# Gate and up of a SwiGLU as 2x2 block products by Strassen's seven, in a float32 decoder layer on one core

## The chip, the core and the metric

The kernel runs on one core of a Trainium2 chip. TensorE (PE) multiplies, VectorE (DVE), ScalarE (ACT) and GpSimd (POOL) work beside it, SyncE (SP) issues most loads. The metric is the device time of one execution in microseconds; lower is better. The inputs are float32 and lie in the chip's main memory; so does the output.

## What is computed

One layer of a decoder on 256 tokens with 2048 columns: a SwiGLU with half weight, a mixer (four heads of differential attention, four of an mLSTM), a second SwiGLU with half weight, and a final norm. The change is in the two SwiGLUs and in what stands around them:

```python
def rmsnorm(x, g):
    x32 = x.astype(jnp.float32)
    y = x32 * lax.rsqrt(jnp.mean(x32 * x32, axis=-1, keepdims=True) + EPS)
    return (y * g.astype(jnp.float32)).astype(x.dtype)

def swiglu(h, w_gate, w_up, w_down):
    return (jax.nn.silu(h @ w_gate) * (h @ w_up)) @ w_down

# in reference(), with D_MODEL = 2048, D_FF = 5632:
x = x + 0.5 * swiglu(rmsnorm(x, ffn1_norm[l]), ffn1_w_gate[l], ffn1_w_up[l], ffn1_w_down[l])
...
x = x + jnp.concatenate([y_a, y_b], axis=-1) @ w_out[l]
x = x + 0.5 * swiglu(rmsnorm(x, ffn2_norm[l]), ffn2_w_gate[l], ffn2_w_up[l], ffn2_w_down[l])
return rmsnorm(x, final_norm)
```

## The kernel before

**Products.** PE multiplies float32 in float32r, a narrower form. To keep the accuracy, each operand is split in two: a high half, cast by ACT (`wh`, L112), and a low half, the rest, subtracted by DVE (`wl`, L113). A product is then three matmuls (`mm3`, L138 to L141): high by high, high by low, low by high. All three add into one PSUM tile `acc` of 128 tokens x 512 columns.

**Tiling.** `linear` computes both token halves of `x @ w` for 512 columns (a chunk). The 2048 rows of the weight are 16 contraction tiles of 128. They are loaded four at a time (1 MB, `raw`, by SP, L125) and split two at a time: a unit, 128 x 1024 elements for ACT and for DVE, is used by twelve matmuls (two contraction tiles, two token halves, three each). A gate chunk and an up chunk are 16 units, 192 matmuls. There are 11 chunks for each of the two SwiGLUs.

**The SwiGLU.** `swiglu` runs over the 11 chunks: gate (`ag`), Silu on ACT (`sg`), up (`au`), and on DVE `hidv`, the gated hidden rows of 128 tokens (L246). These must be transposed before they can be the stationary side of the down product. `hid_transposes` does that on PE (`tr`, eight transposes, L227), splits the result (`hidh` on ACT, `hidl` on DVE) and keeps all 44 transposed tiles until the down product, which runs over four chunks of 512 columns with 44 contraction tiles each and adds to `xres`, the residual.

**The order around the change.** Transposes are put off: they go on a list, `pending`, and `linear` calls `flush()` ahead of its unit FLUSH = 3, so that the last chunk's transposes come in one run between the units of the next product. The program is written in a straight line, and a scheduler places the instructions of each engine by priorities: what stands under `tc.high_priority(offset=AHEAD)` (loads and splits) may come up to 400 places ahead of its use, as far as tiles are free. From then on each engine has one fixed list. The tiles come from pools that rotate: three `raw` tiles, three pairs of `wh` and `wl`, four `acc`, 22 for the hidden halves.

**The head.** In the first chunk, x arrives transposed in eight pieces (`xraw`, L266), each with its split times the norm's gain (`split_gain`, L107 and L108) into `xt0h` to `xt3l`. The two loads of `xres` (L273) come after them. Where x changes later, `chunk_to_xt` transposes it on PE (L210) and splits it.

The functions that the change touches, and what calls them, with the line numbers of the profile:

Of the kernel before, what the change touches and what calls it, by code (L numbers as in the profile page):

```python
# [9 lines left out]
F32 = mybir.dt.float32  # L10
# [34 lines left out]
def tile_trunk_layer(ctx: ExitStack, tc: tile.TileContext, x, xt, par, bias_if, lamv, fnorm,  # L45
# [9 lines left out]
    ps_acc = ctx.enter_context(tc.tile_pool(name="ps_acc", bufs=4, space=PSUM))  # L55
    ps_tr = ctx.enter_context(tc.tile_pool(name="ps_tr", bufs=2, space=PSUM))
    ps_mx = ctx.enter_context(tc.tile_pool(name="ps_mx", bufs=2, space=PSUM))
# [8 lines left out]
    # constants  # L66
# [8 lines left out]
    for _ in range(WARM):  # L75
        # raises TensorE's clock while the first loads are under way
        nc.tensor.matmul(warm, zeros[:, 0:P], zeros, start=True, stop=True)
# [27 lines left out]
    def split_gain(src, gcol, hi, lo):  # L105
        """hi + lo = src * gain, each of float32r's width."""
        nc.scalar.activation(hi, src, AF.Copy, scale=prm[:, gcol:gcol + 1])  # L107
        nc.vector.scalar_tensor_tensor(lo, src, prm[:, gcol:gcol + 1], hi.bitcast(F32),  # L108
                                       op0=ALU.mult, op1=ALU.subtract)
# [9 lines left out]
    def load_w(src, pieces):  # L119
        """one load of LK contraction tiles of w, in pieces"""  # L120
# [17 lines left out]
    def mm3(acc, lh, ll, rh, rl, first, last):  # L138
        nc.tensor.matmul(acc, lh, rh, start=first, stop=False)  # L139
        nc.tensor.matmul(acc, lh, rl, start=False, stop=False)  # L140
        nc.tensor.matmul(acc, ll, rh, start=False, stop=last)  # L141
# [3 lines left out]
    def flush():  # L145
        """the transposes put off into the following products, where they come in one run"""
# [4 lines left out]
    def linear(xp, w, nk, last_units=1, ahead=None, in_pieces=False):  # L151
        """Both token halves of x @ w, w in units of UK contraction tiles, loaded LK at a time;
        xp[kt // 4] are pairs of [P, 4, S] tiles. The first half ends ahead of the second by last_units units."""
# [3 lines left out]
        def products(hb, u, rh, rl):  # L157
            sl = slice(hb * P, (hb + 1) * P)
            for t in range(UK):
                k = u * UK + t  # L160
                xh, xl = xp[k // 4]
                mm3(accs[hb], xh[:, k % 4, sl], xl[:, k % 4, sl], rh[:, t, :], rl[:, t, :],
                    k == 0, k == nk - 1)
# [3 lines left out]
        for u in range(nu):  # L167
# [5 lines left out]
            if o == 0:  # L173
                raw = load_w(w[u * UK // LK], (LK,) if not in_pieces else (UK, UK) if u else (1, 1, UK))
# [10 lines left out]
    def rsq(ssum, n, div, name):  # L185
        """(ssum / div + eps) ** -0.5 on [P, n]"""
# [6 lines left out]
    def square_sum(src, acc, scale=1.0):  # L193
        j = work.tile([P, CW], F32, tag="junk", name=nm("junk"), bufs=1)
# [7 lines left out]
    def chunk_to_xt(c, gbase, xp):  # L202
        """Transposes x's columns of chunk c into xp[c], times the norm's gain."""
        hi, lo = pair_tiles(big, f"xt{c}", [P, 4, S])
        xp[c] = (hi, lo)
        for j in range(0, 4, 2):
# [6 lines left out]
            for i in range(2):  # L213
                split_gain(tr[:, i, :], gbase + 4 * c + j + i, hi[:, j + i, :], lo[:, j + i, :])

    def residual(accs, c, scale, parts):
        for hb in range(NT):
            xs = xres[:, hb, c * CW:(c + 1) * CW]
            nc.vector.scalar_tensor_tensor(xs, accs[hb], scale, xs, op0=ALU.mult, op1=ALU.add)
            square_sum(xs, parts[:, hb, c:c + 1])  # L220
# [10 lines left out]
    def swiglu(xp, rstd, wg, wu, ahead=None):  # L231
        hid = []
        for c in range(F // CW):
            ag = linear(xp, wg[c], KD, ahead=ahead if c == 0 else None,
                        in_pieces=c == 0 and ahead is not None)
            r = rstd()
            sg = []
            for hb in range(NT):
                s = work.tile([P, CW], F32, tag="sg", name=nm("sg"))
                nc.scalar.activation(s, ag[hb], AF.Silu, scale=r[:, hb:hb + 1])  # L240
                sg.append(s)
            au = linear(xp, wu[c], KD)
            hs = []
            for hb in range(NT):
                h = work.tile([P, CW], F32, tag="hidv", name=nm("hidv"))
                nc.vector.scalar_tensor_tensor(h, au[hb], r[:, hb:hb + 1], sg[hb],  # L246
                                               op0=ALU.mult, op1=ALU.mult)
                hs.append(h)
            hi = hidp.tile([P, 4, S], F32R, tag="hid", name=nm("hidh"))
            lo = hidp.tile([P, 4, S], F32R, tag="hid", name=nm("hidl"))  # L250
# [5 lines left out]
    xp1 = {}  # L256

    def load_xt(u):
        k = u * UK
        c, o = k // 4, k % 4  # L260
        if o == 0:
            xp1[c] = pair_tiles(big, f"xt{c}", [P, 4, S])
        hi, lo = xp1[c]
# [465 lines left out]
```

## Time and profile before

| | |
|---|---|
| median of 3 runs | 1873.09 us (1873.05 to 1874.93) |
| the profiled execution, its span | 1870.5 us |
| PE, busy | 1859.7 us, 8456 instructions |
| DVE, busy | 955.4 us, 1031 instructions |
| ACT, busy | 846.4 us, 1019 instructions |
| POOL, busy | 10.0 us, 29 instructions |
| moved by DMA | 353.00 MB, 189 GB/s |

The span goes from the first instruction to the last in the profiler's record; the run's time has 2.6 us around that. In the chain of work that ended last, each step is followed back to what released it, so the engine with most of the chain is the one whose work sets the end. A row of the timeline gives start, duration, engine, line, operation, and the output tile and its inputs; in square brackets stands how long the engine was idle before, and for what. Matmuls are pipelined: their durations overlap, and the cost of one is the distance from start to start.

### The profile page before, as it was taken

Reading aid. Unit: us, or ns where it says so; the run is one execution under the profiler, and the core shown is the slowest. Engines: PE = TensorE matmul, PEld = TensorE weight load, DVE = VectorE, ACT = ScalarE, POOL = GpSimd, SP = SyncE. Lnnn points to the kernel's source line nnn. Section 1 sums busy time; section 2 is a strip of 40 time slices with the busy share of each in tenths; the row PEclk is TensorE's granted clock in tenths of the full one; section 3 lists DMA queues with packets and bytes.
Section 4 is the critical chain, followed back from the end, with each engine's and each line's share of the span. In section 5 each row is a group of like instructions: output and inputs, shape, how many; then the busy total and the mean of one; then the engine's idle time right before and its main releaser. Section 6 shows DMA issues by size and latency. Waiting matters only on the chain.

```text
span 1870.5 us, 20799 instructions
## 1 busy us (share of the span) xinstructions
PE 1859.7 (99%) x8456; PEld 1541.9 (82%) x8456; DVE 955.4 (51%) x1031; ACT 846.4 (45%) x1019; POOL 10.0 (1%) x29
## 2 busy tenths in 40 slices
PE   9999999999999999999999999999999999999998
PEld 7888888888888888978888888888888888888886
DVE  5455444545444454664465555444554445444554
ACT  7444444444444444554455554444444444434443
POOL 0000000000000000000000000000000000000000
PEclk9999999999999999999999999999999999999999
DMA  8555555555555555544544555555555555655553
GB/s 317 197 185 189 193 184 198 181 197 190 184 199 183 200 181 176 189 155 173 185 155 158 182 181 189 192 184 199 181 196 186 190 192 184 221 182 201 186 197 135
DMA packets 51935, 353.00 MB, mean 189 GB/s; under 512 B 6016, under 2 KB 6016, under 8 KB 11136
## 3 DMA queue, kind: packets, MB, share of 16 engines
q1 hardware_dynamic: 50544, 349.26, 51.9%
q10 hardware_dynamic: 1296, 2.42, 0.4%
q8 instruction: 66, 1.08, 0.2%
q14 instruction: 29, 0.24, 0.0%
HBM read 349.56 MB, written 2.10 MB: 188 GB/s over the span
## 4 chain that ended last, share of the span: by engine, by line
PE 98%; DMA 0%; ACT 0%; issue 0%; DVE 0%; POOL 0%; SPq 0%; POOLq 0%
PE acc L139 32%; PE acc L141 32%; PE acc L140 32%; PE tr L227 1%; PE tr L210 0%; DMA xraw<-in_xt_dram 0%; PE sc L547 0%; PE num L513 0%; PE tr L586 0%; PE tr L336 0%; PE rr L471 0%; PE tr L386 0%; PE st L480 0%; PE rr L473 0%; ACT junk L195 0%
## 5 line engine op out<-in xcount | busy, mean ns | idle before, releaser
L113 DVE TENSOR_TENSOR wl<-raw,wh 128x1024 fp32r<-128x1024 f32 (+2 forms) x665 | 805.0, 1211 | 872.8 <-ACT wh L112 872.3
L112 ACT CAST wh<-raw 128x1024 fp32r<-128x1024 f32 (+2 forms) x665 | 693.1, 1042 | 964.3 <-PE acc L141 955.4
L139 PE MATMUL acc<-wh,hidh 128*128 128x512 f32 x704 | 274.3, 390 | 0.0
L141 PE MATMUL acc<-wh,hidl 128*128 128x512 f32 x704 | 273.9, 389 | 0.0
L140 PE MATMUL acc<-wl,hidh 128*128 128x512 f32 x704 | 273.9, 389 | 0.0
L139 PE MATMUL acc<-wh,xt1h 128*128 128x512 f32 (+3 forms) x456 | 178.9, 392 | 0.0
L139 PE MATMUL acc<-wh,xt0h 128*128 128x512 f32 (+3 forms) x456 | 177.4, 390 | 0.3 <-ACT wh L112 0.2
L141 PE MATMUL acc<-wh,xt1l 128*128 128x512 f32 (+3 forms) x456 | 176.6, 387 | 0.0
L140 PE MATMUL acc<-wl,xt0h 128*128 128x512 f32 (+3 forms) x456 | 176.4, 387 | 0.0
L140 PE MATMUL acc<-wl,xt1h 128*128 128x512 f32 (+3 forms) x456 | 176.2, 386 | 0.0
L140 PE MATMUL acc<-wl,xt2h 128*128 128x512 f32 (+3 forms) x456 | 175.9, 386 | 0.0
L141 PE MATMUL acc<-wh,xt0l 128*128 128x512 f32 (+3 forms) x456 | 175.9, 386 | 0.0
L139 PE MATMUL acc<-wh,xt2h 128*128 128x512 f32 (+3 forms) x456 | 175.8, 386 | 0.0
L141 PE MATMUL acc<-wh,xt2l 128*128 128x512 f32 (+3 forms) x456 | 175.8, 386 | 0.0
L139 PE MATMUL acc<-wh,xt3h 128*128 128x512 f32 (+3 forms) x456 | 175.7, 385 | 0.0
L141 PE MATMUL acc<-wh,xt3l 128*128 128x512 f32 (+3 forms) x456 | 175.7, 385 | 0.0
L140 PE MATMUL acc<-wl,xt3h 128*128 128x512 f32 (+3 forms) x456 | 175.7, 385 | 0.0
L141 PEld LDWEIGHTS acc<-wh,hidl 128*128 128x128 f32 x704 | 132.2, 188 | 27.4
L139 PEld LDWEIGHTS acc<-wh,hidh 128*128 128x128 f32 x704 | 132.2, 188 | 27.3
L140 PEld LDWEIGHTS acc<-wl,hidh 128*128 128x128 f32 x704 | 132.2, 188 | 27.2
L139 PEld LDWEIGHTS acc<-wh,xt0h 128*128 128x128 f32 x456 | 85.7, 188 | 18.5 <-ACT wh L112 1.5
L140 PEld LDWEIGHTS acc<-wl,xt0h 128*128 128x128 f32 x456 | 85.7, 188 | 17.7 <-DVE wl L113 1.1
(199 smaller groups left out, 1575.5 us busy)
## 6 DMA issues: line engine op xcount, KB each, us to landing
raw<-in_wu_dram SPq DMA_DIRECT2D x88, 1024.0 KB, 4.8
raw<-in_wd_dram SPq DMA_DIRECT2D x88, 1024.0 KB, 4.8
raw<-in_wg_dram SPq DMA_DIRECT2D x84, 1024.0 KB, 4.8
raw<-in_win_dram SPq DMA_DIRECT2D x40, 1024.0 KB, 4.8
raw<-in_wout_dram SPq DMA_DIRECT2D x16, 1024.0 KB, 4.8
raw<-in_wg_dram SPq DMA_DIRECT2D x7, 512.0 KB, 7.7
raw<-in_wqk_dram SPq DMA_DIRECT2D x4, 784.0 KB, 4.4
raw<-in_wqk_dram SPq DMA_DIRECT2D x4, 768.0 KB, 4.4
```

What stands on the lines that cost most here:

```text
L112: nc.scalar.copy(hi, src)
L113: nc.vector.tensor_tensor(out=lo, in0=src, in1=hi.bitcast(F32), op=ALU.subtract)
L139: nc.tensor.matmul(acc, lh, rh, start=first, stop=False)
L140: nc.tensor.matmul(acc, lh, rl, start=False, stop=False)
L141: nc.tensor.matmul(acc, ll, rh, start=False, stop=last)
L227: nc.tensor.transpose(tr[:, i, hb * P:(hb + 1) * P], hs[hb][:, (j + i) * P:(j + i + 1) * P], ident)
```

## The change

Two contraction tiles (a pair) of x, by its two token halves, are taken as a 2x2 matrix of blocks A1, B1 (first tile) and A2, B2 (second tile); gate's and up's weights for these tiles are another. Their product, a 2x2 matrix too (two token halves by gate and up), is made by Strassen's scheme in Winograd's form: seven block products in place of eight, with four sums of x (`sums`, made once for a SwiGLU), four sums of the weights for each pair and chunk, and sums of the results. NP = 4 pairs, half of the 16 contraction tiles, are done so; the other eight remain plain. The first chunk of the first SwiGLU stays with `linear`.

In `paired`, a pair's gate and up tiles come by two loads of 512 KB into one `raw` tile. DVE makes two of the four weight sums into `f` (L305, 128 x 1024) and one into `raw` (L307, 128 x 512); the fourth is added by a DMA from SBUF to SBUF that accumulates (L354), issued by POOL. Four result tiles stay in PSUM, partial results are added on DVE and ACT (L338 to L341, L383, L386, L387). The SwiGLU's inner 5632 go in three parts of 4, 4 and 3 chunks: gate and up of a part, then its down product with 16, 16 and 12 contraction tiles, which adds to `xres` each time. Pools: 24 `slots` for hidden halves, x, its sums and `f` together, nine work tiles, four `raw`, four pairs of `wh` and `wl`, six `acc` (those of the mixer now among them).

PE's order within a paired chunk is: for each pair a unit u0 and a unit u1 of six matmuls (`prod0`, `prod1`); two units T of six, gate's second tile of two pairs times A2, each split in two pieces of 512; four units S of six, whose split reads the accumulated sum; and eight plain units of twelve, gate's contraction tiles 8 to 15, then up's, with loads of 1 MB.

The core of the diff; T, the plain units and what follows in the mixer (names of pools) are left out:

```diff
 UK = 2
+NP = 4
+PARTS = (4, 4, 3)
...
-    hidp = ctx.enter_context(tc.tile_pool(name="hidp", bufs=22))
-    wr = ctx.enter_context(tc.tile_pool(name="wr", bufs=3))
-    wsp = ctx.enter_context(tc.tile_pool(name="wsp", bufs=3))
-    work = ctx.enter_context(tc.tile_pool(name="work", bufs=2))
+    slots = ctx.enter_context(tc.tile_pool(name="slots", bufs=24))
+    work = ctx.enter_context(tc.tile_pool(name="work", bufs=9))
+    wr = ctx.enter_context(tc.tile_pool(name="wr", bufs=4))
+    wsp = ctx.enter_context(tc.tile_pool(name="wsp", bufs=4))
...
+    def sums(g):
+        for o, a, b, op in ((S1, B1, B2, ALU.subtract), (S3, A1, B1, ALU.subtract),
+                            (S2, S1, A1, ALU.subtract), (S4, A2, S2, ALU.add)):
+            nc.vector.tensor_tensor(out=g[:, o, :], in0=g[:, a, :], in1=g[:, b, :], op=op)
...
+    def paired(xp, wa, wb, nk, after_a):
+        n11, n21, n12, n22 = (ps_acc.tile([P, CW], F32, tag="acc", name=nm("acc")) for _ in range(4))
+        p1, p7, p5, p6 = n11, n21, n12, n22
...
+        def sums_first(j):
+            k = 2 * j
+            raw = wr.tile([P, 4, CW], F32, tag="raw", name=nm("raw"))
+            with tc.high_priority(offset=AHEAD):
+                nc.sync.dma_start(raw[:, 0:2, :], wa[k // LK][:, k % LK:k % LK + 2, :])
+                nc.sync.dma_start(raw[:, 2:4, :], wb[k // LK][:, k % LK:k % LK + 2, :])
+                f = slots.tile([P, 2, CW], F32, tag="s", name=nm("f"))
+                nc.vector.tensor_tensor(out=f, in0=raw[:, 0:4:3, :],
+                                        in1=raw[:, 2:3, :].to_broadcast([P, 2, CW]), op=ALU.add)
+                nc.vector.tensor_tensor(out=raw[:, 2, :], in0=f[:, 0, :], in1=raw[:, 3, :], op=ALU.add)
+                u0 = pair_tiles(wsp, "w", [P, 2, CW])
+                split(raw[:, 0:3:2, :], *u0)
+                u1 = pair_tiles(wsp, "w", [P, 2, CW])
+                split(f, *u1)
+            raws.append(raw)
+            return u0, u1
...
+        for j in range(NP):
+            if j == 2:
+                flush()
+            u0, u1 = sums_first(j)
+            prod0(j, u0)
+            held.append((j, u1))
+            if j != NP - 2:
+                for h in held:
+                    prod1(*h)
+                held.clear()
+        u2, u3, v = wk("u2"), wk("u3"), wk("v")
+        with soon():
+            nc.scalar.copy(u3, p1)
+            nc.vector.tensor_tensor(out=u2, in0=p6, in1=u3, op=ALU.add)
+            nc.vector.tensor_tensor(out=u3, in0=p7, in1=u2, op=ALU.add)
+            nc.vector.tensor_tensor(out=v, in0=p5, in1=u3, op=ALU.subtract)
...
+        for j in range(NP):
+            raw = raws[j]
+            with tc.high_priority(offset=AHEAD):
+                nc.gpsimd.dma_start(raw[:, 2, :], raw[:, 1, :], accum_op=ALU.add)
+                t = pair_tiles(wsp, "w", [P, 2, CW])
+                split(raw[:, 2:4, :], *t)
+            prod(n21, xp["pair", j], B2, t, 0, False, False, True)
+            prod(n12, xp["pair", j], S4, t, 1, False, False, True)
...
+    def ffn(xp, rstd, wg, wu, wd, finish, first=None):
+        done = 0
+        for part, n in enumerate(PARTS):
+            hid = hidden(xp, rstd, wg, wu, range(done, done + n), first)
+            for c in range(4):
+                finish(c, functools.partial(linear, dict(enumerate(hid)), wd[c], n * 4, w0=done), part,
+                       part == len(PARTS) - 1)
+            done += n
...
     def load_xt(u):
...
+            if u < NP:
+                g = gained(raw, G_FFN1 + k)
+                hi, lo = sum_tiles(xp1, u)
+                split(g[:, 0:4, :], hi[:, 0:4, :], lo[:, 0:4, :])
+                gs.append((g, hi, lo))
...
+        if u >= KD // UK - NP:
+            g, hi, lo = gs.pop(0)
+            sums(g)
+            split(g[:, 4:8, :], hi[:, 4:8, :], lo[:, 4:8, :])
```

**What moves.** The first place is DVE's list around the transposes of the last chunk's hidden rows. Before, in the second chunk of the first SwiGLU: the two `hidv`, four units of the weight, the two low halves of the transposes, the next unit.

```order
L246 SCALAR_TENSOR_TENSOR hidv_74_497<-acc_52_359,rstd_49_353,sg_50_355 128x512
L246 SCALAR_TENSOR_TENSOR hidv_75_499<-acc_53_360,rstd_49_353,sg_51_357 128x512
L113 TENSOR_TENSOR wl_87_542<-raw_85_539,wh_86_541 128x1024
L113 TENSOR_TENSOR wl_91_572<-raw_85_539,wh_90_571 128x1024
L113 TENSOR_TENSOR wl_94_590<-raw_92_587,wh_93_589 128x1024
L113 TENSOR_TENSOR wl_96_606<-raw_92_587,wh_95_605 128x1024
L113 TENSOR_TENSOR hidl_77_502<-tr_88_557,hidh_76_501 128x512
L113 TENSOR_TENSOR hidl_77_502<-tr_89_564,hidh_76_501 128x512
L113 TENSOR_TENSOR wl_99_624<-raw_97_621,wh_98_623 128x1024
```

After, in its fourth chunk: the two gated rows (`hv`), pair 1's second unit, the first low half, then the sums of pairs 2 and 3 (`f_247` and `raw_246`, `f_253` and `raw_252`), the second low half, pair 2's first unit.

```order
L278 SCALAR_TENSOR_TENSOR hv_224_1219<-u2_187_1001,rstd_57_383,sg_212_1145 128x512
L278 SCALAR_TENSOR_TENSOR hv_225_1221<-v_189_1003,rstd_57_383,sg_213_1147 128x512
L114 TENSOR_TENSOR wl_243_1266<-f_239_1258,wh_242_1265 128x1024
L114 TENSOR_TENSOR hidl_227_1224<-tr_244_1281,hidh_226_1223 128x512
L305 TENSOR_TENSOR f_247_1298<-raw_246_1295 128x1024
L305 TENSOR_TENSOR f_253_1318<-raw_252_1315 128x1024
L307 TENSOR_TENSOR raw_246_1295<-f_247_1298,raw_246_1295 128x512
L307 TENSOR_TENSOR raw_252_1315<-f_253_1318,raw_252_1315 128x512
L114 TENSOR_TENSOR hidl_227_1224<-tr_245_1288,hidh_226_1223 128x512
L114 TENSOR_TENSOR wl_249_1302<-raw_246_1295,wh_248_1301 128x1024
```

Between the low half of `tr_244` and that of `tr_245` now stand four sums that the next matmuls need; before, the two stood together, and the units ahead of them were those that PE used around its transposes.

The second place is PE's list at the same transposes. Before, from the fourth transpose to the first two matmuls of the unit behind them:

```order
L227 MATMUL tr_88_557<-ident_103,hidv_75_499 128x128
L227 MATMUL tr_89_564<-ident_103,hidv_74_497 128x128
L227 MATMUL tr_89_564<-ident_103,hidv_75_499 128x128
L227 MATMUL tr_89_564<-ident_103,hidv_74_497 128x128
L227 MATMUL tr_89_564<-ident_103,hidv_75_499 128x128
L139 MATMUL acc_78_503<-wh_90_571,xt1h_12_184 128x512
L140 MATMUL acc_78_503<-wl_91_572,xt1h_12_184 128x512
```

After, in the same way; `acc_228`, `acc_231` and `acc_229` are three of the chunk's four result tiles:

```order
L264 MATMUL tr_244_1281<-ident_100,hv_225_1221 128x128
L264 MATMUL tr_245_1288<-ident_100,hv_224_1219 128x128
L264 MATMUL tr_245_1288<-ident_100,hv_225_1221 128x128
L264 MATMUL tr_245_1288<-ident_100,hv_224_1219 128x128
L264 MATMUL tr_245_1288<-ident_100,hv_225_1221 128x128
L141 MATMUL acc_228_1225<-wh_248_1301,xs_18_191 128x512
L141 MATMUL acc_231_1228<-wh_248_1301,xs_18_191 128x512
L141 MATMUL acc_229_1226<-wh_250_1305,xs_18_191 128x512
L142 MATMUL acc_228_1225<-wl_249_1302,xs_18_191 128x512
```

The transposes stand between units as before, but what follows them (`wh_248`, `wh_250`) is now split from sums that DVE's list has behind the transposes' low half.

The third place is SP's list of loads in the first chunk. Before, its last x pieces and what follows:

```order
L266 DMA xraw_27_260<-in_xt_dram 128x512
L125 DMA raw_33_291<-in_wg1_dram 128x1024
L266 DMA xraw_32_284<-in_xt_dram 128x512
L125 DMA raw_33_291<-in_wg1_dram 128x1024
L266 DMA xraw_36_310<-in_xt_dram 128x512
L125 DMA raw_54_361<-in_wu1_dram 128x2048
L125 DMA raw_59_395<-in_wu1_dram 128x2048
L273 DMA xres_128<-in_x_dram 128x2048
L125 DMA raw_64_429<-in_wu1_dram 128x2048
L273 DMA xres_128<-in_x_dram 128x2048
```

After, from the first load of up's weights to the last x piece:

```order
L126 DMA raw_62_391<-in_wu1_dram 128x2048
L431 DMA xraw_23_214<-in_xt_dram 128x512
L126 DMA raw_67_425<-in_wu1_dram 128x2048
L452 DMA xres_125<-in_x_dram 128x2048
L431 DMA xraw_29_239<-in_xt_dram 128x512
L126 DMA raw_72_459<-in_wu1_dram 128x2048
L431 DMA xraw_35_272<-in_xt_dram 128x512
L431 DMA xraw_38_300<-in_xt_dram 128x512
L452 DMA xres_125<-in_x_dram 128x2048
L126 DMA raw_77_493<-in_wu1_dram 128x2048
L431 DMA xraw_44_334<-in_xt_dram 128x512
```

Up's weights (`in_wu1`) and x itself (`xres`) came behind the last piece of `xraw`; now four loads of the one and both of the other stand among and ahead of the pieces.

More of the change, by code (lines that the diff above doesn't have):

```diff
@@ L136, in split_w, with mm3, halves @@
         return hi, lo
[L138 to L141, printed above, removed]
+    def mm3(acc, lh, ll, rh, rl, first, last, on=False):
+        nc.tensor.matmul(acc, lh, rh, start=first, stop=False, skip_group_check=on)
+        nc.tensor.matmul(acc, lh, rl, start=False, stop=False, skip_group_check=on)
+        nc.tensor.matmul(acc, ll, rh, start=False, stop=last, skip_group_check=on)
+    def halves(xp, k, hb):
+        if ("pair", k // 2) in xp:
+            xh, xl = xp["pair", k // 2]
+            i = 2 * (k % 2) + hb
+            return xh[:, i, :], xl[:, i, :]
+        xh, xl = xp[k // 4]
+        sl = slice(hb * P, (hb + 1) * P)
+        return xh[:, k % 4, sl], xl[:, k % 4, sl]
     pending = []
@@ L229, in hid_transposes, with wk @@
             split(tr, hi[:, j:j + 2, :], lo[:, j:j + 2, :])
-    def swiglu(xp, rstd, wg, wu, ahead=None):
-        hid = []
[L233 to L250, printed above, removed]
+    def wk(name):
+        return work.tile([P, CW], F32, tag="w", name=nm(name))
@@ new lines, in hidden @@
+    def hidden(xp, rstd, wg, wu, chunks, first=None):
+        hid = []
+        for c in chunks:
+            if c == 0 and first is not None:
+                ag = linear(xp, wg[c], KD, ahead=first, in_pieces=True)
+                r = rstd()
+                sg = [gate(ag[hb], r[:, hb:hb + 1]) for hb in range(NT)]
+                au = linear(xp, wu[c], KD)
+            else:
+                sg = []
+                r = rstd()
+                au = paired(xp, wg[c], wu[c], KD,
+                            lambda ag: sg.extend(gate(ag[hb], r[:, hb:hb + 1]) for hb in range(NT)))
+            with soon():
+                hs = [gated(au[hb], r[:, hb:hb + 1], sg[hb]) for hb in range(NT)]
+            hi = slots.tile([P, 4, S], F32R, tag="s", name=nm("hidh"))
+            lo = slots.tile([P, 4, S], F32R, tag="s", name=nm("hidl"))
```

171 lines of the change are left out of this document (127 added, 44 removed).

## The prediction

> **What bounds the kernel now.** I read the busy shares first, then the chain that ended last, then one gate-and-up chunk out of 22 in the windows and the timeline. Busy time and the engines' shares of the chain:
>
> ```profile
> PE 1859.7 (99%) x8456; PEld 1541.9 (82%) x8456; DVE 955.4 (51%) x1031; ACT 846.4 (45%) x1019; POOL 10.0 (1%) x29
> PE 98%; DMA 0%; ACT 0%; issue 0%; DVE 0%; POOL 0%; SPq 0%; POOLq 0%
> ```
>
> PE sets the time: it stands for 98% of the chain, and DVE is idle half of the time. Next, the transposes of two neighbouring chunks in the chain, a window (PE, PEld, DVE, ACT and POOL busy, granted clock, DMA share, GB/s), and two matmuls that begin one unit of twelve apart:
>
> ```profile
> 281.69 0.87 PE tr L227 x8
> 326.11 0.87 PE tr L227 x8
> ...
> 272.60:317.00 44.40, 44.40 (x202) 36.86 (x201) 22.11 (x21) 19.12 (x20) 0.00 (x0) 1.00 0.52 190
> ...
> 300.10 0.39 PE L139 MATMUL acc<-wh,xt0h 128*128 128x512 f32 x1
> 302.82 0.39 PE L139 MATMUL acc<-wh,xt1h 128*128 128x512 f32 x1
> ```
>
> A chunk takes 44.42 us, PE is busy in all of it, and a matmul costs 2.72 / 12 = 0.2267 us: 192 of them are 43.5, the eight transposes 0.87. So matmuls taken away are worth their full price as long as PE stays fed. Whether it does is a question to DVE and ACT, whose prices are these (count, busy us, mean ns, idle time before and its cause):
>
> ```profile
> L113 DVE TENSOR_TENSOR wl<-raw,wh 128x1024 fp32r<-128x1024 f32 x639 | 782.6, 1225 | 849.9 <-ACT wh L112 849.4
> L112 ACT CAST wh<-raw 128x1024 fp32r<-128x1024 f32 x639 | 673.5, 1054 | 943.2 <-PE acc L141 935.2 <-issue 3.4 <-DVE xt3l L108 1.7
> L113 DVE TENSOR_TENSOR hidl<-tr,hidh 128x512 fp32r<-128x512 f32 x44 | 28.2, 682 | 0.0
> L112 ACT CAST hidh<-tr 128x512 fp32r<-128x512 f32 x44 | 23.5, 586 | 0.0
> ```
>
> The time from start to start is shorter than these durations. DVE's and PE's timeline:
>
> ```profile
> 316.35 1.23 DVE L113 TENSOR_TENSOR wl<-raw,wh 128x1024 fp32r<-128x1024 f32 x1 [1.49 <-ACT wh L112]
> 317.49 1.40 DVE L246 SCALAR_TENSOR_TENSOR hidv<-acc,rstd,sg 128x512 f32<-128x512 f32 x2
> 319.07 1.23 DVE L113 TENSOR_TENSOR wl<-raw,wh 128x1024 fp32r<-128x1024 f32 x1 [0.18 <-ACT wh L112]
> ...
> 327.23 1.23 DVE L113 TENSOR_TENSOR wl<-raw,wh 128x1024 fp32r<-128x1024 f32 x1 [1.50 <-ACT wh L112]
> 328.37 1.28 DVE L113 TENSOR_TENSOR hidl<-tr,hidh 128x512 fp32r<-128x512 f32 x2
> ...
> 325.95 1.04 PE L227 MATMUL tr<-ident,hidv 128*128 128x128 f32 x8
> ```
>
> Back to back, 1024 elements take DVE 1.14 us (317.49 - 316.35; 328.37 - 327.23), 512 some 0.60 (two in 1.28). The order of the trace is that of DVE's list, and at 327.23 DVE stood idle for 1.50 us for a cast without taking anything ahead: I take DVE as strictly in order.
>
> **The change: what it saves.** Each of the four pairs of contraction tiles has seven products of three matmuls instead of eight, 21 for 24: a paired chunk has 180 matmuls instead of 192. 21 chunks x 12 x 0.2267 us = 57.1 us, all of it on PE's path. In three parts, the down product has the same matmuls; its 32 more residual additions (0.68 us each by the 512-element rows) fall where DVE is half idle, and are hidden by PE's 2.72 us a unit against DVE's 1.14.
>
> **What it adds to DVE.** Per paired chunk 24 operations of 1024 elements and 18 of 512: 24 x 1.14 + 18 x 0.60 = 38.2 us, against a PE time of 180 x 0.2267 + 0.87 = 41.7. That is 92%: on average DVE still fits, but it has 3.5 us left for everything it waits for. Before, it was 22.1 of 44.4.
>
> **Where it waits.** The order after the change puts on DVE, between the two low halves of the hidden transposes, all four sums of pairs 2 and 3 (L305, L305, L307, L307). Those two halves need the transposes, which PE does only after the products of pairs 0 and 1. So nothing for pairs 2 and 3 can be made ready in advance. With t = 0 at the chunk's first matmul:
> - PE: 24 matmuls to 5.44, the first four transposes to 5.9, all to 6.31. DVE has done the last chunk's ends and pair 1's split by 3.5 and stands idle.
> - ACT casts hidh from 6.1 (0.59). DVE: hidl starts at 6.73, f2 at 7.33, f3 at 8.47, the raw sum of pair 2 at 9.61 to 10.30, of pair 3 at 10.21, the second hidl to 11.5.
> - ACT casts pair 2's first unit from 10.34 to 11.39 (1.05). PE's next matmul starts at 11.44: **5.1 us idle**.
> - DVE's four low halves of pairs 2 and 3 end at 12.7, 13.8, 14.9, 16.1; PE has 24 matmuls (5.44 us) here but ends them at about 18.6 rather than 16.9: 1.8 us more.
> - T to 21.3. DVE has no gap from 6.7 to the last S split, (11 x 0.60 + 10 x 1.14 = 18.0) at 24.8; S starts when the first S split is there (21.5) and ends at 26.9. The first plain unit's load can be issued only when S0's split (21.5) has freed its raw tile; its price is the 4.8 us of a 1 MB load:
>
> ```profile
> raw<-in_wu_dram SPq DMA_DIRECT2D x88, 1024.0 KB, 4.8
> raw<-in_wg_dram SPq DMA_DIRECT2D x7, 512.0 KB, 7.7
> out_dram<-xres SPq DMA_DIRECT2D x4, 256.0 KB, 3.0
> ```
>
> so it lands at 26.3, is cast by 27.4 and split by 28.6: 1.4 us idle. The plain units then run at PE's 2.72.
>
> That is 8.3 us idle in a chunk of 41.7: 50.0 against 44.4. It holds for 17 chunks: those with hidden transposes in this place (all paired ones but the first of the second and third part of each layer), and the second layer's first, where transposes of x stand there. Bounds: the single durations of that path, with no latency between, are hidh 0.59 + hidl 0.60 + two sums 2.28 + raw sum 0.69 + cast 1.05 = 5.2 from the fourth transpose, of which PE fills 0.43 with the other four: 4.8 us at least before pair 2. The other two waits (1.8, 1.4) may be half as long: low end 6.4. If the plain load lands like the 512 KB rows, 2.9 us later: high end 11.2. In the 4 other chunks the sums stand early in DVE's queue, and only the plain load's wait is left, 0.6 each.
>
> **The head.** In the order after the change SP issues all four first loads of wu and both loads of x itself ahead of the last x piece. Before, it issued none of them there. SP's fifth x piece before, PE's first product on it, the landing time of such pieces, and a window of that time:
>
> ```profile
> 7.60 0.43 SPq L266 DMA_DIRECT2D xraw<-in_xt_dram  x1
> 18.56 0.39 PE L139 MATMUL acc<-wh,xt2h 128*128 128x512 f32 x1
> ...
> xraw<-in_xt_dram SPq DMA_DIRECT2D x8, 256.0 KB, 7.3
> ...
> 14.00:18.00 4.00, 4.00 (x19) 3.31 (x18) 4.00 (x7) 3.83 (x8) 0.00 (x0) 1.00 1.03 402
> ```
>
> The DMA engines are full (share 1.03, 402 GB/s). 6 MB come ahead of the last piece: 6.3 / 0.402 = 15.6 us late. PE can fill 2 x 2.72 of it with wu units whose data are there, and a piece was 18.56 - 7.60 - 7.3 = 3.7 us early: 15.6 - 5.4 - 3.7 = 6.5, which I take; ends 0 and 15.6.
>
> **The accumulating DMA.** 84 of them on POOL's queue, 256 KB each inside SBUF. The trace has none; the nearest is the 256 KB store, 3.0 us. Pair 3's goes out at about 15.0, when its raw sum has been read, and its sum is needed at 21.4: 6.4 us of cover. I take 0, by that row; nothing waits less for it, so the ends are 0 and, at 10 us, 3.6 x 21 = 76.
>
> **Sum,** against the profiled execution: 1870.5 - 57.1 + 17 x 8.3 (141.1) + 4 x 0.6 (2.4) + 6.5 = 1963.4. The span lies 2.6 us below the median of the runs (1873.09), which I keep: **1966 us, 5.0% slower**. Its own range goes from 17 x 6.4 and no head loss (1927) to 17 x 11.2 (2015).
>
> **Rivals.**
>
> *The clock falls in the idle time.* At the end of the kernel PE's last matmul begins at 1861.75 (0.39 long). The clock granted after it, and the products on zeros at the start:
>
> ```profile
> 1866.00:1867.00 1.00, 0.00 (x0) 0.00 (x0) 0.00 (x0) 0.00 (x1) 0.00 (x0) 1.00 1.00 367
> 1867.00:1868.00 1.00, 0.00 (x0) 0.00 (x0) 0.00 (x0) 0.00 (x0) 0.00 (x0) 0.63 1.04 330
> 1868.00:1869.00 1.00, 0.00 (x0) 0.00 (x0) 0.00 (x0) 0.00 (x0) 0.00 (x0) 0.50 0.93 350
> ...
> 1.25 4.45 PE L77 MATMUL warm<-zeros 128*128 128x512 bf16 x10 [1.25 <-DVE touch L72]
> ```
>
> A mean of 0.63 puts the fall to one half at 1867.26, 5.1 us after PE stopped: exactly my idle time, so it can go either way. At half clock a matmul takes 0.445 us, and ten of them pass before the clock is back: 10 x 0.218 = 2.2 us, of which up to 1.8 are spent waiting for the low halves anyway. 0.4 to 2.2 a chunk, 1.6 taken: 17 x 1.6 = 27, 1993 us. Chance 0.28. The Trainium skill, "TensorE: Matmul & The Clock Gate" (Why this matters for your kernels), speaks against the change here: it wants no gap above some 3 us between bursts of matmuls, since one idle window halves the clock. By that rule all 17 chunks lose it, and the sum is that of this rival; the trace's own fall came later than that, after 5.1 us.
>
> *The accumulating DMA lands late.* For it: no DMA of the trace is issued by POOL, so its issue itself has no row. Against: the cover is twice the nearest row. At 8 us 21 x 1.6 = 34, 2000 us; at 10 us 2042. Chance 0.10.
>
> *Faster.* If the sums of pairs 2 and 3 were done before the transposes (DVE passes over a waiting hidl, or its 3.2 us of idle time before it is used), 41.7 us a chunk would be left: 1870.5 - 57.1 + 6.5 + 2.4 + 2.6 = 1825 us. It decides where the idle time per flush chunk stays below (57.1 - 6.5 - 2.4) / 17 = 2.8 us. Even with DVE at half its durations the 4.8 only fall to 0.59 + 0.30 + 1.14 + 0.35 + 1.05 - 0.43 = 3.0. Against it stands the in-order row at 327.23. Chance 0.04.
>
> *The stalls just eat the saving* (2.8 us a chunk): 1873; chance 0.02.
>
> **How the numbers follow.** The forecast has 0.56, the clock 0.28, the DMA 0.10, faster 0.04, no change 0.02. Some 0.2% is what can be told from no change here. 1932 leaves out the two last cases and the lowest end of the forecast's own range, 2010 the top of that range and the worst of the clock and of the late DMA: together under 0.2. Slower by over 0.2%: 0.56 + 0.28 + 0.10 = 0.94; same 0.02, faster 0.04.
>
> **What the profile after would show.** PE's busy share falls to some 92% ((1859.7 - 57.1) / 1963), with 252 matmuls fewer. Chunks with transposes last about 50 us, the others 41.4. PE's longest idle time stands right behind the hidden transposes, about 5 us, put down to ACT's wh; DVE is idle for about 3 us before hidl and then runs for 18 us without a gap. L305 should read near 1225 ns, L307 near 690. The accumulating DMA shows its landing time: above 6.4 us means PE waits before S. Granted clock: under 1.00 in the windows behind the idle time, if the rival is right. The prediction is wrong if DVE's queue runs its sums before 6.7 us of the chunk, or if the idle time before pair 2 is far from 5 us.

## The result, and the profile after

The change makes the kernel slower: 2049.3 us (2046.46 to 2052.27, four runs) against 1873.07; the ratio is 1.094, 95% interval 1.0925 to 1.0956. The prediction had the side, and was 83 us short. The page's busy shares and the engines' shares of the chain, of the changed kernel:

```profile
PE 1909.6 (93%) x8204; PEld 1517.8 (74%) x8204; DVE 1343.7 (66%) x1553; ACT 990.7 (48%) x1218; POOL 81.6 (4%) x113
PE 82%; DVE 9%; DMA 4%; ACT 3%; issue 2%; SPq 0%; DVEq 0%; ACTq 0%; POOLq 0%; POOL 0%
```

PE has 252 instructions fewer, as computed, but is busy 50 us longer, and DVE, ACT and DMA now have a part in the chain. Where the time went is seen by stages, each from its first product in PE's timeline to the next stage's first (us):

| stage | before | after | difference |
|---|---|---|---|
| gate and up, first SwiGLU | 489.6 | 217.4 + 196.3 + 144.9 = 558.6 | +69.1 |
| down, both | 483.0 | 500.4 | +17.4 |
| mixer, up to its output product | 303.8 | 332.1 | +28.3 |
| output product | 90.7 | 93.1 | +2.4 |
| gate and up, second SwiGLU | 488.7 | 205.1 + 195.4 + 144.8 = 545.3 | +56.5 |

The forecast was +92.9 for gate and up, and nothing elsewhere. Now one chunk with transposes, its pieces of the chain in order of time without PE's own products (start, us, what), and the windows of such a chunk and of one stretch without transposes:

```profile
127.34 0.45 PE tr L264 x4
...
127.81 0.59 ACT hidh L113
...
129.03 2.35 DVE f L305 x2
131.39 0.61 DVE raw L307
...
132.06 1.05 ACT wh L113
...
143.53 4.83 DMA raw<-in_wg_dram
...
148.46 1.06 ACT wh L113
...
149.55 1.24 DVE wl L114
```

```profile
121.60:172.90 51.30, 45.79 (x190) 35.70 (x189) 39.12 (x43) 25.89 (x29) 3.39 (x4) 0.93 0.55 185
216.00:258.00 42.00, 42.00 (x186) 33.89 (x185) 22.94 (x23) 16.64 (x17) 0.00 (x0) 1.00 0.52 185
```

DVE's timeline in the same chunk, its first and its last rows ahead of the plain units:

```profile
128.43 0.69 DVE L114 TENSOR_TENSOR hidl<-tr,hidh 128x512 fp32r<-128x512 f32 x1 [3.44 <-ACT hidh L113]
129.03 2.35 DVE L305 TENSOR_TENSOR f<-raw 128x1024 f32<-128x1024 f32 x2
...
142.28 4.62 DVE L114 TENSOR_TENSOR wl<-raw,wh 128x1024 fp32r<-128x1024 f32 x4
```

That is the path which the prediction laid out: transposes, hidh, hidl, the sums, the cast, and later the plain load that waited for the raw tile. The 17 chunks with transposes last 51.2 us in the mean (50.8 to 52.2; 50.0 foretold), PE is idle for 5.6 of it, and the mean granted clock is 0.93 in twelve of them and 0.97 in five. Next, PE's rows on which the rest turns: in the down product, two matmuls that begin twelve apart; in the mixer's scans; and in the head.

```profile
285.16 0.39 PE L141 MATMUL acc<-wh,hidh 128*128 128x512 f32 x1
287.96 0.39 PE L141 MATMUL acc<-wh,hidh 128*128 128x512 f32 x1
...
872.43 0.58 PE L625 MATMUL mg<-ident,gcol 128*4 128x128 f32 x2 [5.80 <-DVE gcol L619]
882.62 0.27 PE L643 MATMUL mmc<-ident,mrow 4*128 4x4 f32 x1 [9.61 <-DVE mrow L637]
...
13.50 0.50 PE L141 MATMUL acc<-wh,xs 128*128 128x512 f32 x1 [3.75 <-ACT xs L113]
21.02 0.50 PE L141 MATMUL acc<-wh,xs 128*128 128x512 f32 x1 [2.97 <-ACT xs L113]
28.23 0.61 PE L141 MATMUL acc<-wh,xs 128*128 128x512 f32 x1 [2.59 <-ACT xs L113]
```

Twelve matmuls take 2.80 us here and took 2.72 before: 0.2333 us each at a granted clock of 1.00, in a product that the change doesn't touch. In the mixer PE waits 15 us for DVE's scans, which stood beside products before. In the head it waits four times behind its first product for x's halves: the three rows shown, and 1.54 us at 34.80.

### The profile page after: what moved, and what is told of

It reads as the page before. It is cut to its first block, busy times and chain, and to the rows that moved or that the text cites. A ratio compares the mean times of both kernels' runs of the same rounds, so it can differ in the third digit from the quotient of the medians.

```text
span 2045.3 us, 21792 instructions
## 1 busy us (share of the span) xinstructions
PE 1909.6 (93%) x8204; PEld 1517.8 (74%) x8204; DVE 1343.7 (66%) x1553; ACT 990.7 (48%) x1218; POOL 81.6 (4%) x113
## 4 chain that ended last, share of the span: by engine, by line
PE 82%; DVE 9%; DMA 4%; ACT 3%; issue 2%; SPq 0%; DVEq 0%; ACTq 0%; POOLq 0%; POOL 0%
PE acc L142 26%; PE acc L141 26%; PE acc L143 26%; DMA raw<-in_wg_dram 4%; DVE wl L114 3%; ACT wh L113 2%; DVE f L305 2%; PE tr L264 1%; DVE raw L307 1%; DVE u L340 1%; DVE u L339 1%; ACT hidh L113 0%; DVE cv L542 0%; DVE v L341 0%; PE tr L221 0%
## 5 line engine op out<-in xcount | busy, mean ns | idle before, releaser
L142 PE MATMUL acc<-wl,xt 128*128 128x512 f32 (+3 forms) x1120 | 438.4, 391 | 9.5 <-DVE wl L114 9.4
L141 PE MATMUL acc<-wh,xt 128*128 128x512 f32 (+3 forms) x1120 | 436.1, 392 | 3.7 <-ACT wh L113 1.7
L143 PE MATMUL acc<-wh,xt 128*128 128x512 f32 (+3 forms) x1120 | 435.6, 389 | 0.0
L141 PE MATMUL acc<-wh,xs 128*128 128x512 f32 x620 | 257.0, 430 | 95.8 <-ACT wh L113 85.0
L142 PEld LDWEIGHTS acc<-wl,xt 128*128 128x128 f32 x1120 | 210.6, 188 | 63.8 <-DVE wl L114 18.5
L142 PE MATMUL acc<-wl,xs 128*128 128x512 f32 x620 | 257.7, 416 | 0.1
L143 PE MATMUL acc<-wh,xs 128*128 128x512 f32 x620 | 256.2, 414 | 0.4 <-DVE xs L114 0.4
L141 PEld LDWEIGHTS acc<-wh,xt 128*128 128x128 f32 x1120 | 209.2, 188 | 57.0 <-ACT wh L113 9.7
L143 PEld LDWEIGHTS acc<-wh,xt 128*128 128x128 f32 x1120 | 210.5, 188 | 46.5 <-DVE xt L109 0.5
L141 PEld LDWEIGHTS acc<-wh,xs 128*128 128x128 f32 x620 | 124.1, 204 | 137.2 <-ACT wh L113 97.0
L143 PEld LDWEIGHTS acc<-wh,hidl 128*128 128x128 f32 x704 | 132.0, 187 | 32.3
L142 PEld LDWEIGHTS acc<-wl,xs 128*128 128x128 f32 x620 | 123.1, 199 | 35.6 <-DVE wl L114 6.8
L143 PEld LDWEIGHTS acc<-wh,xs 128*128 128x128 f32 x620 | 124.0, 200 | 29.5 <-DVE xs L114 1.4
L354 POOL DMA_DIRECT2D raw<-raw x84 | 71.6, 852 | 1416.7 <-DVE wl L114 1386.3
L113 ACT CAST wh<-f 128x1024 fp32r<-128x1024 f32 x84 | 87.9, 1046 | 69.9 <-PE acc L143 68.2
```

Source lines behind the costliest of these rows:

```text
L113: nc.scalar.copy(hi, src)
L141: nc.tensor.matmul(acc, lh, rh, start=first, stop=False, skip_group_check=on)
L142: nc.tensor.matmul(acc, lh, rl, start=False, stop=False, skip_group_check=on)
L143: nc.tensor.matmul(acc, ll, rh, start=False, stop=last, skip_group_check=on)
L354: nc.gpsimd.dma_start(raw[:, 2, :], raw[:, 1, :], accum_op=ALU.add)
```

## The experiments

Each one is told with its edit. Times are medians; a ratio is that to the kernel before on the same chip, with its 95% interval.

**The matmul's step: a few bytes of padding.** The mixer's tiles for m_v have 2 x 257 numbers, 2056 bytes. In the changed kernel they share the nine work tiles, which so take 2080 bytes each, and everything behind them, wh and wl too, moves by 32 bytes modulo 256 (9 x 2080 = 18720). The same two lines went into the changed kernel (a1_pad) and into the one before (a2_padbefore):

```diff
+    pad = ctx.enter_context(tc.tile_pool(name="pad", bufs=1)).tile([P, 8], F32, name="pad32")
     wr = ctx.enter_context(tc.tile_pool(name="wr", bufs=4))
...
+    nc.vector.memset(pad, 0.0)
```

> The changed kernel with 32 bytes of padding ahead of the raw, wh and wl tiles, which moves the start of wh and wl from 32 past a multiple of 64 bytes to a multiple of 64; nothing else differs. Theory A (the moving tile's start sets the matmul's cost): start-to-start of the 512-column matmuls goes back from 0.2333 to 0.2267 us, some 8000 matmuls x 6.7 ns = 53 us less, about 1996 us. Theory B (the longer step comes from six PSUM tiles, four buffers or a busier DVE): it stays at 0.2333, 2049 us.

> The kernel before with the same 32 bytes of padding, which here moves wh and wl away from a multiple of 64 bytes. Theory A: 0.2333 us for a matmul, some 8260 x 6.7 ns = 55 us more, about 1928 us. Theory B: 0.2267 us and 1873 us as before.

a2_padbefore took 1921.67 us, ratio 1.0261 (1.0245 to 1.0276): 32 bytes cost the old kernel 48.6 us. Its step in the down product, twelve matmuls again (2.80):

```profile
599.85 0.40 PE L141 MATMUL acc<-wh,hidh 128*128 128x512 f32 x1
602.65 0.40 PE L141 MATMUL acc<-wh,hidh 128*128 128x512 f32 x1
```

a1_pad took 2028.91 us (1.0825, 1.0807 to 1.0843), and its step only fell to 0.2290. A miss for the simple theory: a multiple of 64 bytes is not enough. Seven more runs, six of the old kernel with other paddings and one of the changed kernel with the mixer's four tiles moved to the pool of the large ones (e_align), settled what is:

```diff
 # b_pad64, e_mov128, e_mov256: 64, 128, 256 bytes ahead of raw, wh and wl
+    pad = ctx.enter_context(tc.tile_pool(name="pad", bufs=1)).tile([P, 16], F32, name="pad32")
     wr = ctx.enter_context(tc.tile_pool(name="wr", bufs=3))
 # e_all32: 32 bytes ahead of everything large; d_stat32: so, and 224 more ahead of raw; d_stat64: 64 and 192
+    pad = ctx.enter_context(tc.tile_pool(name="pad", bufs=1)).tile([P, 8], F32, name="pad")
     big = ctx.enter_context(tc.tile_pool(name="big", bufs=1))
 # e_align, in the changed kernel
-        if math.prod(shape[1:]) <= 2 * (VD + 1):
+        if math.prod(shape[1:]) <= 2 * VD:
```

> The kernel before with 64 bytes of padding ahead of raw, wh and wl, so that wh and wl start at a multiple of 128 bytes while x's and the hidden tiles still start 64 past one, as in the changed kernel with 32 bytes of padding. Theory A (a multiple of 64 bytes is all that the moving tile needs): 0.2267 us a matmul, 1873 us. Theory B (where the moving tile lies against the stationary one counts too: with 32 bytes the changed kernel's matmuls of the high halves kept 0.2333): one matmul in three is 6.7 ns longer, 8260 x 6.7 / 3 = 18 us more, 1891 us.

> The kernel before with x's and the hidden tiles (the stationary side, and xres) moved by 32 bytes, and wh and wl by 256, which leaves their place against multiples of 256 as it was. Theory A (only the moving side's start counts): 0.2267 us a matmul, 1873 us. Theory B (a start off a multiple of 64 bytes costs on either side): 0.2333 us, 1873 + 49 as with the moving side moved by 32 = 1922 us.

> The kernel before with x's and the hidden tiles moved by 64 bytes, to a multiple of 128, and wh and wl by 256 as in the last one: moving and stationary side lie 64 bytes apart again, the other way round than with 64 bytes of padding. Theory A (the cost of that padding came from the moving side's own start at a multiple of 128): 1873 us. Theory B (it came from where the two lie against each other): 1873 + 16 = 1889 us.

> The kernel before with every large tile, stationary and moving, moved by 32 bytes. Theory A (each side must start at a certain place, 64 past a multiple of 128 or the like): 0.2333 us a matmul, 1922 us. Theory B (what counts is the distance between the moving and the stationary tiles, here a multiple of 512 as before): 0.2267 us, 1873 us.

> The kernel before with raw, wh and wl moved by 128 bytes. Theory A (the start, modulo 128): 1873 us. Theory B (the distance, modulo 512): slower, by 16 us as with 64 bytes or by 49 as with 32: 1889 to 1922 us.

> The kernel before with raw, wh and wl moved by 256 bytes, the shift that two earlier runs had in them. Theory A (the start, modulo 128 or 256): 1873 us. Theory B (the distance, modulo 512): slower, 1889 to 1922 us.

> The changed kernel with the mixer's four odd-sized tiles moved to another pool, so that wh and wl start where they did before the change, and nothing else. 0.2267 us a matmul. Theory A (in the chunks with transposes only the plain units gain, since DVE sets the rest): 17 x 96 + 4 x 180 + 192 + 2112 + 384 + 1248 = 6300 matmuls x 6.7 ns = 42 us less, 2007 us. Theory B (all 8100 count): 54 us less, 1995 us.

The distance is that from x's and the hidden tiles (stationary) to wh and wl (moving), in bytes modulo 256, worked out from the sizes of the pools (the profile shows no addresses); the step is the mean from one 512-column matmul to the next in PE's timeline, good to some 0.0002 us:

| kernel | distance mod 256 | step, us | time, us | ratio |
|---|---|---|---|---|
| before | 0 | 0.2268 | 1873.07 | 1 |
| a2_padbefore | 32 | 0.2333 | 1921.67 | 1.0261 (1.0245 to 1.0276) |
| b_pad64 | 64 | 0.2290 | 1889.87 | 1.0079 (1.0062 to 1.0096) |
| e_mov128 | 128 | 0.2326 | 1917.43 | 1.0240 (1.0225 to 1.0255) |
| d_stat64 | 192 | 0.2333 | 1922.01 | 1.0258 (1.0241 to 1.0275) |
| d_stat32 | 224 | 0.2333 | 1921.51 | 1.0254 (1.0238 to 1.0269) |
| e_mov256 | 0 | 0.2268 | 1873.21 | 1.0005 (0.9996 to 1.0015) |
| e_all32 | 0 | 0.2268 | 1872.65 | 1.0004 (0.9994 to 1.0013) |
| changed | 32 | 0.2333 | 2049.30 | 1.0940 (1.0925 to 1.0956) |
| a1_pad | 64 | 0.2290 | 2028.91 | 1.0825 (1.0807 to 1.0843) |
| e_align | 0 | 0.2269 | 2019.66 | 1.0784 (1.0768 to 1.0800) |

So it is the distance, and not where either side starts: with both moved by 32 bytes nothing happens, with one of them moved the step grows, and a distance of 256 is as good as none. Two expectations missed on the way: d_stat64 had 1873 or 1889 us and took 1922, and e_mov256 shows that the modulus is not 512. Other tiles moved along (raw with wh and wl, xres with x), so that the two sides of the matmul are what counts is the reading that fits, not a thing tried alone. Why 64 bytes cost a third of what 32 cost while 192, as far the other way, cost as much as 32, and why the two sides get in each other's way at all, was not tried.

e_align gave 29.6 us back, less than either theory, since the chunks with transposes still took 51.1 us in the mean. Their plain units did get shorter (22.7 us for 23.3), but the stretch from PE's restart behind the transposes to the first plain unit, which DVE's list sets, got longer by nearly as much (16.9 us for 16.4). Why it did was not followed.

**The transposes out of DVE's way** (a3_flush):

```diff
-            if j == 2:
-                flush()
...
+                if w is wa and k == 2 * NP + UK:
+                    flush()
```

> The changed kernel with the hidden transposes put off to the second plain unit of a chunk, so that DVE's sums of pairs 2 and 3 no longer stand behind the transposes' low half. A flush chunk lasts 51.4 us now, of which 42.9 are PE's work at its present pace. Theory A (the 5 us wait and the half clock after it cost the chunk 8.5 us): all but the wait for the first plain load, some 1 us, goes: 17 x 7.5 = 128 us less, 1921 us. Theory B (DVE at 92% has no room, and the wait comes up elsewhere): the chunk stays above 46 us and no more than half is won, 1985 us or more.

1956.41 us, ratio 1.0445 (1.0429 to 1.0460): 93 us less. In DVE's timeline of one such chunk, where the changed kernel had idle time of 3.44 us ahead of the first hidl, pair 3's sums now follow the splits without a wait, and the hidden low halves come last:

```profile
388.53 1.22 DVE L114 TENSOR_TENSOR wl<-f,wh 128x1024 fp32r<-128x1024 f32 x1
389.67 1.22 DVE L305 TENSOR_TENSOR f<-raw 128x1024 f32<-128x1024 f32 x1
390.92 0.69 DVE L307 TENSOR_TENSOR raw<-f,raw 128x512 f32<-128x512 f32 x1
392.84 1.22 DVE L114 TENSOR_TENSOR wl<-raw,wh 128x1024 fp32r<-128x1024 f32 x1 [1.23 <-ACT wh L113]
...
403.86 1.28 DVE L114 TENSOR_TENSOR hidl<-tr,hidh 128x512 fp32r<-128x512 f32 x2
```

Most of these chunks last 45.8 us, with PE idle for 1.8: the place of the transposes was worth some 5.4 us a chunk, but with four pairs a chunk is still longer than the 44.4 of before. That lies between the two theories: more than half of the first one's 128 us was won, but the chunk stays hardly below the second one's 46 us.

**The clock in the idle time** (a4_fill):

```diff
+                fill = ps_tr.tile([P, CW], F32, tag="tr", name=nm("fill"))
+                for _ in range(14):
+                    nc.tensor.matmul(fill, zeros[:, 0:P], zeros, start=True, stop=True)
```

> The changed kernel with 14 matmuls on zeros behind the hidden transposes of every flush chunk, into a spare transpose tile, so that PE is not idle for 5 us in one piece; order and waits of the other engines are as in the changed kernel. Theory A (the half clock after the idle time costs about 3 us a chunk): the granted clock stays at 1.00 and the time falls by 17 x 3 = 51 us, to about 1998. Theory B (PE would wait for DVE's low halves there anyway): the clock stays at 1.00, but at most 1.2 us a chunk are won, 2029 us or more.

2048.23 us, 1.0935 (1.0918 to 1.0951): nothing, although the clock was kept. The windows after the transposes, two of the changed kernel, then two of a4_fill (the granted clock is the third number from the end), and the filling itself:

```profile
131.00:133.00 2.00, 0.00 (x0) 0.00 (x0) 2.00 (x4) 0.94 (x1) 0.00 (x0) 0.50 0.00 0
133.00:135.00 2.00, 1.84 (x4) 1.37 (x5) 2.00 (x3) 2.00 (x4) 0.33 (x1) 0.50 0.00 0
```

```profile
134.00:136.00 2.00, 1.19 (x6) 0.49 (x4) 2.00 (x4) 1.40 (x2) 0.00 (x0) 1.00 0.00 0
136.00:138.00 2.00, 1.78 (x8) 1.13 (x7) 2.00 (x3) 2.00 (x3) 0.80 (x1) 1.00 0.00 0
...
131.71 3.18 PE L331 MATMUL fill<-zeros 128*128 128x512 bf16 x14 [0.96 <-DVE hidl L114]
```

DVE is busy for all of these windows. PE at half speed just fills time that it would have spent waiting for DVE. The chunks last 51.2 us in the mean with the full clock and without. Their medians are 51.0 and 51.3, so the half clock may cost some 0.25 us a chunk, 4 us in all, which is less than the runs of one kernel differ here.

**The mixer's PSUM tiles** (b_mix):

```diff
-    ps_acc = ctx.enter_context(tc.tile_pool(name="ps_acc", bufs=6, space=PSUM))
+    ps_acc = ctx.enter_context(tc.tile_pool(name="ps_acc", bufs=4, space=PSUM))
+    ps_mx = ctx.enter_context(tc.tile_pool(name="ps_mx", bufs=2, space=PSUM))
...
-        rr = ps_acc.tile([P, CW], F32, tag="acc", name=nm("rr"))
+        rr = ps_mx.tile([P, CW], F32, tag="mx", name=nm("rr"))
```

> The changed kernel with PSUM split as before the change: four tiles for products, two of their own for the mixer's small results. Read by the mixer's stage (from the first product on wqk to the first on wout), 332.1 us in the changed kernel against 303.8 before. Theory A (in the shared ring of six, the tiles of m_v's products come behind those of the decays, so that PE's list has nothing to do while DVE runs the scans): the stage falls to about 303.8 + 7.6 for the slower matmuls = 311 us. Theory B (the other pools, or slower work on DVE): it stays near 332. In the paired chunks four tiles cost a wait at each chunk's start, about 1 us x 21, so the whole may not get faster: 2030 to 2050 us.

2028.42 us in two runs (1.0821, 1.0800 to 1.0843). The mixer's stage falls from 332.1 to 313.7 us, and the two idle times of 5.80 and 9.61 us are gone. The merged ring was their cause: a tile for m_v's product could only be had after those of the decays. The wait that four accumulators were expected to cost the paired chunks did not come: those with transposes last 51.3 us in the mean.

**The head's loads** (b_head):

```diff
+    def load_x(u):
+        if u < KD // UK and u not in xr:
+            xr[u] = slots.tile([P, UK, S], F32, tag="s", name=nm("xraw"))
+            with tc.high_priority(offset=AHEAD):
+                nc.sync.dma_start(xr[u], xt[:, u * UK:u * UK + UK, :])
...
+        for v in range(u, u + 4):
+            load_x(v)
+        raw = xr[u]
```

> The changed kernel with the pieces of transposed x issued three units ahead, so that they stand ahead of the loads of up's weights in SP's list, as before the change. Read by the time to the first down product, 217.4 us after its start in the changed kernel, 12.2 us more than the same stage of the second SwiGLU. Theory A (PE waits there for late x pieces): 205 us, 2037 us in all. Theory B (ACT and DVE, which split x and its sums, are the limit in the head): above 213 us.

2033.38 us in two runs (1.0848, 1.0826 to 1.0869); the stage takes 201.95 us instead of 217.40. In PE's timeline only this is left of the waits in the head behind the first product:

```profile
12.13 0.73 PE L141 MATMUL acc<-wh,xs 128*128 128x512 f32 x2 [0.34 <-ACT xs L113]
15.81 0.50 PE L141 MATMUL acc<-wh,xs 128*128 128x512 f32 x1 [0.21 <-ACT xs L113]
```

The time is theory A's, but its reason is not what the changed kernel's trace shows. ACT's timeline ahead of the products at 21.02 and 28.23, which are those on the third and the fourth piece, and the landing times of the pieces:

```profile
18.09 1.04 ACT L113 CAST wh<-raw 128x1024 fp32r<-128x1024 f32 x1 [2.74 <-PE acc L143]
19.04 0.90 ACT L239 ACTIVATE xg<-xraw,prm 128x256 f32<-128x256 f32 x2
...
25.67 1.04 ACT L113 CAST wh<-raw 128x1024 fp32r<-128x1024 f32 x1 [2.49 <-PE acc L143]
26.62 0.90 ACT L239 ACTIVATE xg<-xraw,prm 128x256 f32<-128x256 f32 x2
...
DMA to landing us min/median/max: 3.1/9.7/10.8
```

SP issued these pieces at 6.63 and 11.94, so they had landed by 17.4 and 22.7. What came late was ACT: in its list a cast of weights (`wh`), which waits until PE has done with an earlier unit, stands ahead of the piece's gain (`xg`), and PE then waits for that piece. The wait at 34.80 has the same form (a cast after 3.62 us of waiting for PE, then the piece that was issued at 16.66). The last piece, issued at 36.00, made PE wait for nothing: its last wait in this chunk ends at 39.31, for a `wh`. In b_head, where the loads are issued earlier, ACT's list changed too: it does not wait for PE until 25.28, when all eight pieces have their gain. What each of the two orders is worth was not told apart.

**All causes out, two pairs or four** (c_np2, c_np4). Both have the edits of a3_flush, b_head and e_align, and m_v's two products moved between the mixer's scans; c_np4 leaves NP at 4:

```diff
-NP = 4
+NP = 2
...
+    mv_chunk(0)
     bcol = ct([P, 20], "bcol")
...
+    mv_chunk(1)
     sc = [ct([NH, NT, 64 + P], f"scan{i}") for i in range(2)]
```

> The changed kernel with the causes taken out: two pairs instead of four (186 matmuls a chunk), so that raw tiles are free for the plain loads and DVE has time to spare; transposes put off to the plain units; x pieces ahead; m_v's products between the steps of the mixer's scans; the odd-sized tiles moved, so that wh and wl start where they did before the change. Theory A (these were the costs, and the saved matmuls then count in full): 21 x 6 x 0.2267 = 28.6 us less than before, with some 5 us given back for the down products in parts and the head: about 1850 us. Theory B (the sums still make PE wait in each chunk, 1.4 us or more): 1873 us or more.

> The kernel with the causes taken out, but with four pairs as in the change. Theory A (four raw tiles are all held by the pairs, and DVE has some 3 us to spare in a chunk, so the wait for the first plain load stays): chunks with transposes take 44.8 us (45.8 with the transposes moved alone, 180 x 6.7 ns = 1.2 less at most), against 43.1 with two pairs: 17 x 1.7 - 4 x 1.2 = 24 us more than with two pairs, 1872 us. Theory B (the last waits came from the other causes): 41.8 us a chunk, 21 x 1.36 = 29 us less than with two pairs, 1819 us.

c_np2 takes 1847.78 us (1844.88 to 1851.64), ratio 0.9859 (0.9843 to 0.9875): it beats both kernels, and comes out where theory A put it (1850). Its busy shares and one chunk:

```profile
PE 1830.9 (99%) x8330; PEld 1518.4 (82%) x8330; DVE 1193.5 (65%) x1371; ACT 923.0 (50%) x1128; POOL 46.0 (2%) x71
...
313.10:356.20 43.10, 43.10 (x195) 35.70 (x194) 32.27 (x35) 22.78 (x25) 1.70 (x2) 1.00 0.60 207
```

PE is busy in all of the chunk's 43.1 us, and DVE in 32.3. c_np4 takes 1885.61 (1.0062, 1.0046 to 1.0077): most of its chunks with transposes last 45.3 us with some 1.9 idle, and the whole is 14 us slower than theory A had. The idle times are of the kinds foreseen, for the low halves and for the first plain load:

```profile
382.51 0.50 PE L142 MATMUL acc<-wl,xs 128*128 128x512 f32 x1 [0.63 <-DVE wl L114]
388.50 0.74 PE L141 MATMUL acc<-wh,xt 128*128 128x512 f32 x2 [0.71 <-ACT wh L113]
389.76 0.51 PE L142 MATMUL acc<-wl,xt 128*128 128x512 f32 x1 [0.53 <-DVE wl L114]
```

So 12 matmuls fewer in a chunk don't pay where the sums take DVE's time and the raw tiles, and 6 fewer do.

## Why the prediction was right on the side and wrong on the size

- *What is saved:* right. 252 matmuls are gone, and where nothing waits, a matmul less is worth its step (c_np2: 43.1 us for 186 matmuls and 8 transposes, 43.0 by the old step).
- *Where DVE waits:* right, nearly row by row. PE resumed 11.56 us after the chunk's start (133.16 - 121.6; 11.44 foretold, and 11.44 measured with e_align's step) after 4.95 us idle (5.1); DVE ran from hidl at 128.43 to the last S split at 146.9, 18.5 us (18.0), with one gap of 0.30; the plain load took 4.83 (4.8). Most of the 1.8 us of waiting for low halves showed as a slower clock instead. 51.2 us for 50.0: 21 us over 17 chunks, 2 of them by the longer step (51.1 with e_align). In the rows the excess lies at the plain units: their load went out 21.95 us after the start for 21.5, its low half was ready at 29.2 for 28.6, and the eight units took 23.3 us for 21.8.
- *The accumulating DMA:* right. It lands in 3.3 us, and no wait on it appears.
- *The clock:* the fall came in every one of these chunks, the cost did not (a4_fill). The rival's step that failed is that the half speed costs what DVE's low halves don't hide. The Trainium skill, "TensorE: Matmul & The Clock Gate" (Why this matters for your kernels), wants no gap above some 3 us; the trace agrees on the fall, in the chunk shown 2.7 us after PE's last transpose (128.21 to 130.9, from a mean clock of 0.93 between 130 and 131), but hardly any time hung on it here.
- *The head:* that PE would wait there was right, the mechanism and the size were not: 6.5 us for the last piece, which cost nothing, where b_head gave 15.9. PE waited for the second to the fifth piece; three of these four had landed by then, and stood in ACT's list behind casts that waited for PE. The clock fell to a half three times in between.
- *The step of the sum that failed* is one that it took without saying: that all matmuls and all stages which the change leaves alone keep their price. The 0.2267 us of "180 x 0.2267" were carried over to tiles in other places, and the mixer stood in no term, though the change's pools merge its PSUM tiles into the products' ring. The runs put 29.6 us on the first (e_align) and 20.9 on the second (b_mix).

Of the 83 us this makes 29.6 + 20.9 + 9.4 (head, 15.9 - 6.5) + 19 (chunks, beside the step) = 79. The other 4 were not told apart. Each of these was measured by itself; that they may be added is borne out by c_np4, which takes 163.7 us off the changed kernel, where the four single runs (a3_flush 92.9, e_align 29.6, b_mix 20.9, b_head 15.9) make 159.3.

## What to carry to other kernels

Work that is saved on the bounding engine is worth its price only if what feeds it is not put behind something that waits: read the fixed order of the feeding engine at the point of the wait, and add up its durations there. A change of pools is a change of its own: it can move a product behind others in a shared ring (20.9 us here), and it can move tiles by a few bytes, in stages that the diff doesn't name (29.6 us). Before a smaller algorithm is given up, a smaller dose of it (two pairs for four) may still win.

## What the runs showed of the hardware

In these runs a float32r matmul of 512 columns with its own weight load takes 0.2268 us from start to start if moving and stationary tile lie a multiple of 256 bytes apart within the partition, 0.2333 at 32, 192 and 224, 0.2326 at 128, and 0.2290 at 64. The step gets up to 2.9% longer, and the kernel before up to 2.6%, at an unchanged granted clock, and matmul durations in the rows (0.39 to 0.40) hardly show it; the distance of their starts does. The granted clock fell 2.0 to 2.9 us after PE's last work in twelve of the 17 chunks, 4.5 to 5.2 us after it in the other five, and 5.1 us after it at the end of the old kernel. In the changed kernel's trace each stretch between two changes of the clock lasts a multiple of 3.41 us (3.41 or 6.83 at half clock in the chunks), which fits a delay that depends on where in such a step PE stops.
